# Fillers in one fp32r pass at both block heads, and block 2's first units in the scheduler's order

## The chip, the cores and the metric

The kernel runs on one core of a Trainium2 chip. The metric is the device time of one execution in microseconds, from its first to its last instruction and the little around it. Engines are named as in the profile: TensorE (PE, with PEld for its weight loads), VectorE (DVE), ScalarE (ACT), GpSimd (POOL) and SyncE (SP), which here only issues DMAs.

## The reference, cut to what matters

512 tokens of 2048 features go through three blocks in a row. Each block normalises, multiplies by a wide weight matrix, mixes the tokens in two ways, and multiplies by an output matrix.

```python
def reference(x, ...):                      # x: [1, 512, 2048], float32
    x = first_block(x, ...)
    x = second_block(x, ...)
    return third_block(x, ...)

def first_block(x, ...):
    h = rms_norm(x, norm_gain)
    z = einsum('bsd,de->bse', h, w_in)      # gated recurrence + dilated attention
    ...
    x = x + einsum('bse,ed->bsd', y, w_out)
    return rms_norm(x, final_gain)

def second_block(x, c, ...):
    shift, scale, gate = split(silu(c) @ w_ada + b_ada, 3)
    h = _layernorm(x) * (1.0 + scale) + shift
    proj = h @ w_in                         # spatial gating + neighbourhood attention
    ...
    x = _layernorm(x + (1.0 + gate) * y, ln_g, ln_b)

def third_block(x, c, ...):
    h = rms_norm_3(x, norm_gain) * (1.0 + scale) + shift
    ... = split(h @ w_in)                   # gated delta rule + sliding-window attention
    ...
    x = x + gate * (mixed @ w_out)
```

The change lies at the two places where one block ends and the next begins: the norm ahead of block 2, and the two norms ahead of block 3.

## The kernel before

**Tiles.** Activations are kept transposed, features on the 128 partitions and the 512 tokens along the row, so 2048 features are KT = 16 feature tiles of 128x512. Inputs and weights are float32. For the wide products each value is split into a high half, rounded to the type fp32r, and a low half, the rest. A weight piece is loaded by SP as `wr`, ACT rounds it to `wh` (L114, the helper `act`), DVE subtracts to get `wl` (L117, the helper `tt`). There are three buffers for `wr` and five each for `wh` and `wl`. An activation tile `a` is a pair (high, low) made in the same way. Each weight tile of 128x128 then takes three products of 128x512 (`mm`, L128): high x high, high x low, low x high. A unit is one 128-feature output tile: 16 feature tiles x 3 products into one PSUM bank `pm`.

**First units.** At the head of a block the activation tiles come one by one, since each must first be normalised. `first_units` (L231 to L279) therefore runs four units at once, tile by tile: when feature tile k is ready, its 4 x 3 products are issued. Only the last four tiles are taken unit by unit. `make(k)` is the work of one tile. For block 2 (L773 to L783) it is: two DVE operations `t <- t, x` with the broadcast norm factors, one ACT operation `t <- t` with the modulation's scale and bias, one on ACT for the high half, and one on DVE for the low half. `first_chunks` issues the loads of the weight pieces for tile k and splits them, through SP, ACT and DVE. `FIRST2 = (8, 0, 16, 9)` and `FIRST3` name the four units.

**Heads of blocks.** `out1` multiplies block 1's result by its output matrix, 16 units. Each unit's tile gets the residual, is normalised by the token means found so far, and is squared for the statistics. The last unit is in `out1_end`: its last products, its tile, sums over features by one-column products against `ones` (`stat_last`), then a chain of small operations on DVE and POOL that gives the norm's factors g and c, then `bcast_cols`, eight products of 128x128 that spread g and c over the partitions into the banks that `make` reads. `out2_end` does the same for block 3 with two norms in one, a longer chain, and three factors.

**Fillers.** In these two stretches TensorE has to wait for the others, and the kernel issues products whose results nobody reads. `warm(n, src)` issues n of them into a bank `x`. With `src = ds[0]`, a normalised float32 tile, each is a float32 product of `ones` and 512 columns. There are three groups at each head: behind the last unit, behind the sums, and behind the broadcasts.

**What sets the order.** Normally a scheduler orders the instructions of each engine by its own estimates. Inside `with self.in_order()` the instructions of DVE, ACT and TensorE stay in the order in which the code is written; SP and POOL are ordered by the scheduler throughout. Before the change, `out1_end` and the first units of block 2 that it calls were both inside (L725 and L726). `out2_end` with the first units of block 3 is inside as well, in both versions.

```python
    def run(self):
        ...
        h, first = self.out1(self.block1())
        h, first = self.out2(self.block2(h, first))
        self.drain_bg()
        self.out3(self.block3(h, first))
```

Of the kernel before, what the change touches and what calls it, by code (L numbers as in the profile page):

```python
# [18 lines left out]
P = 128  # L19
# [15 lines left out]
FIRST2 = (8, 0, 16, 9)  # L35
# [5 lines left out]
class Kernel:  # L41
# [148 lines left out]
    def warm(self, n, src=None):  # L190

        b = self.x()
        src = self.ones if src is None else src
        for _ in range(n):
            self.mm(b[:, 0:src.shape[-1]], self.ones, src)

    def in_order(self):

# [518 lines left out]
    def out1(self, ys):  # L717
        ysp = [self.split(v) for v in ys]
        self.stat_begin(3)
        ds = []  # L720
        self.sc2 = self.cp.tile([P, 32], F32, name="sc2")
        for ct in range(KT - 1):
            self.out1_tile(ct, self.unit(self.A["wo1"], ct, ysp), ds)
        self.ts(self.sc2, self.mod2[:, 16:48], 1.0, None, OP.add)
        with self.in_order():  # L725
            return self.out1_end(ysp, ds)  # L726

    def out1_tile(self, ct, ps, ds):
        nc = self.nc
# [19 lines left out]
    def out1_end(self, ysp, ds):  # L749
        nc = self.nc  # L750
        last, ps = self.last_unit(self.A["wo1"], ysp, self.stat_sum)
        self.warm(5, ds[0])
        lasts = self.out1_tile(KT - 1, last, ds)
        self.stat_last(ps, lasts)
        self.warm(5, ds[0])
        m, v, a, g, c = (self.s(4) for _ in range(5))

        self.ts(a, ps[:, 8:12], LN_EPS / D, LN_EPS * EPS)
        self.ts(m, ps[:, 0:4], 1.0 / D)
        self.stt(v, ps[:, 4:8], 1.0 / D, a, OP.mult, OP.add)  # L760
        self.tt(c, m, m)
        self.tt(v, v, c, OP.subtract)
        nc.gpsimd.tensor_tensor(g, v, self.nhalf[:, :4], OP.pow)
        self.r1 = self.cp.tile([P, 4], F32, name="r1")
        self.ts(a, ps[:, 8:12], 1.0 / D, EPS)
        nc.gpsimd.tensor_tensor(self.r1, a, self.nhalf[:, :4], OP.pow)
        self.stt(c, m, -1.0, g, OP.mult, OP.mult)
        chunks = self.end(self.first_chunks(self.A["w2"], FIRST2, 0))
        gb, cb = self.bcast_cols(g), self.bcast_cols(c)
        self.warm(5, ds[0])  # L770
        mod = self.mod2

        def make(k):  # L773
            t1 = self.t()
            self.tt(t1, ds[k], gb)
            self.tt(t1, t1, cb, OP.add)
            self.act(t1, t1, AF.Identity, scale=self.sc2[:, k:k + 1], bias=mod[:, k:k + 1])
            hi, lo = self.a(), self.a()
            self.act(hi, t1)
            yield  # L780
            yield
            self.tt(lo, t1, hi.bitcast(F32), OP.subtract)
            return hi, lo  # L783

        return self.first_units(self.A["w2"], FIRST2, make, chunks)


    def sgu(self, g, h, w, ys):
# [195 lines left out]
    def out2_end(self, ysp, ds, acc, cf, K, gsc, bsc):  # L984
        nc = self.nc
        mod = self.mod3
        w = self.A["w3"]

        def late():
            st = self.x()  # L990
            for i, a in enumerate(acc):
                for j in range(4):
                    self.mm(st[:, 5 * j + i:5 * j + i + 1], a[:, j * P:(j + 1) * P], self.ones[:, 0:1],
                            start=i == 0 and j == 0, stop=False)
            return st

        last, st = self.last_unit(self.A["wo2"], ysp, late)
        self.warm(4, ds[0])
        d, sq = self.out2_tile(KT - 1, last, ds, acc, cf)
        for v, o, n in ((d, 0, 3), (sq, 3, 2)):  # L1000
            for j in range(4):
                self.mm(st[:, 5 * j + o:5 * j + o + n], v[:, j * P:(j + 1) * P], cf[:, 0:n, KT - 1],
                        start=False, stop=True)
        self.warm(9, ds[0])
        s20 = self.s(20)
        nc.vector.tensor_copy(s20, st[:, 0:20])
        S = [s20[:, i::5] for i in range(5)]
        m, v, q, p, al, be = (self.s(4) for _ in range(6))
        g, c = self.gc3[:, 0:4], self.gc3[:, 4:8]
        self.ts(m, S[0], 1.0 / D)  # L1010
        self.ts(v, S[3], 1.0 / D, LN_EPS)
        self.tt(q, m, m)
        self.tt(v, v, q, OP.subtract)
        nc.gpsimd.tensor_tensor(g, v, self.nhalf[:, :4], OP.pow)

        self.ts(q, q, K[:, 0:1])
        self.tt(q, q, S[4], OP.add)
        self.tt(al, m, S[1])
        self.stt(q, al, -2.0, q, OP.mult, OP.add)
        self.stt(be, m, K[:, 1:2], S[2], OP.mult, OP.subtract)  # L1020
        self.tt(q, q, g)
        self.stt(q, be, -2.0, q, OP.mult, OP.add)
        self.tt(q, q, g)
        self.ts(q, q, K[:, 2:3], None, OP.add)
        nc.gpsimd.tensor_tensor(p, q, self.nhalf[:, :4], OP.pow)
        self.stt(c, m, -1.0, g, OP.mult, OP.mult)
        self.tt(al, g, p)
        self.tt(be, c, p)
        chunks = self.end(self.first_chunks(w, FIRST3, 0))
        rows = [self.k(t) for t in ("acc0", "km", "acc1")]  # L1030
        for r, v in zip(rows, (al, be, p)):
            b = self.bcast_cols(v)
            self.act(r, b)
        self.warm(5, ds[0])
        alb, beb, pb = rows

        def make(k):
            t1 = self.t()
            self.tt(t1, ds[k], alb)
            self.tt(t1, t1, beb, OP.add)  # L1040
            self.act(t1, t1, AF.Identity, scale=gsc[:, k:k + 1], bias=mod[:, k:k + 1])
            yield
            self.stt(t1, pb, bsc[:, k:k + 1], t1, OP.mult, OP.add)
            hi, lo = self.a(), self.a()
            self.act(hi, t1)
            yield
            self.tt(lo, t1, hi.bitcast(F32), OP.subtract)
            return hi, lo

        small = []  # L1050
        for n in range(4):
            small.append(self.x())
        W = 272

        def side(k, h):

            raw = self.t()[:, :W]
            nc.sync.dma_start(raw, self.A["w3s"][:, k * W:k * W + W])
            hi, lo = self.e(F32R)[:, :W], self.e(F32R)[:, :W]
            self.act(hi, raw)  # L1060
            yield
            self.tt(lo, raw, hi.bitcast(F32), OP.subtract)
            yield
            for n in range(4):
                c, o = slice(n * P, (n + 1) * P), small[n][:, :W]
                self.mm(o, h[k][0][:, c], hi, start=k == 0, stop=False)
                self.mm(o, h[k][1][:, c], hi, start=False, stop=False)
                self.mm(o, h[k][0][:, c], lo, start=False, stop=k == KT - 1)

        h, first = self.first_units(w, FIRST3, make, chunks, side)  # L1070
        self.vb = [self.rows1, self.cp.tile([P, T], F32, name="vb1")]
        self.ba = self.cp.tile([P, 64], F32, name="ba")
        for n in range(4):
            nc.vector.tensor_copy(self.ba[:, 16 * n:16 * n + 16], small[n][:, 256:272])
            for i in range(2):
                self.act(self.vb[i][:, n * P:(n + 1) * P], small[n][:, i * P:(i + 1) * P])
        return h, first
# [678 lines left out]
```

## Time and profile before

| | |
|---|---|
| median of 3 runs | 3457.22 us (3456.98 to 3463.95) |
| the profiled execution | 3459.73 us |
| its span, first to last instruction | 3458.0 us |
| its mean granted TensorE clock | 0.996 |
| products of `pm` with `wh`, with `wl` | 8512, 4256 |
| DMA | 451.68 MB, mean 131 GB/s |

The page gives busy time by engine, and a list of the costliest groups of instructions with the idle time ahead of them and the engine that ended it. Busy time alone says little here, since TensorE is nearly always busy, some of it with fillers. The views that matter are the list of waits on TensorE, the busy time by stretches of the span, and the instructions one by one around the two block heads, which lie near 1045 to 1063 us and 1966 to 1985 us. A row such as `pm <- DVE a L117` reads: a product into `pm` waited for the tile `a`, which DVE writes on line 117. Numbers in the order below are buffer numbers of the program; the profile leaves them out.

### The profile page before, as it was taken

What the parts mean: (1) busy time and instruction counts of PE and PEld (TensorE: products, weight loads), DVE (VectorE), ACT (ScalarE), POOL (GpSimd) and SP (SyncE); (2) the same over time, 40 slices, a digit from 0 to 9 for tenths busy, and PEclk for the clock granted to TensorE, in tenths of its full rate; (3) what the DMA queues carried; (4) which work ended last, traced back from release to release, by engine and by line L of the source; (5) the groups of instructions that cost most, each with busy time, mean ns of one, the idle gap of its engine ahead of it and who ended that gap; (6) DMA issues with size and microseconds to landing.
All of it is one profiled execution on the core that took longest, in us unless ns stands there. A gap on an engine that the chain in (4) does not pass through costs nothing.

```text
span 3458.0 us, 44442 instructions
## 1 busy us (share of the span) xinstructions
PE 3408.4 (99%) x16689; PEld 2827.2 (82%) x16689; DVE 1976.9 (57%) x3593; ACT 1278.8 (37%) x2459; POOL 132.8 (4%) x156
## 2 busy tenths in 40 slices
PE   9999999999998999999999999999999999999999
PEld 7877788888885888888888788888888888888887
DVE  8677656657775556644357677756754333344552
ACT  4222244445334222544452243332334443432331
POOL 0000000000000000101000000000000000000000
PEclk9999999999999999999999999999999999999999
DMA  6355445435662355432234233332222233324442
GB/s 220 124 181 177 135 140 178 157 117 185 213 217 93 129 166 200 169 124 90 88 101 144 95 111 106 99 98 84 84 71 84 96 101 104 126 98 146 140 139 96
DMA packets 166168, 451.68 MB, mean 131 GB/s; under 512 B 26496, under 2 KB 47296, under 8 KB 165952
## 3 DMA queue, kind: packets, MB, share of 16 engines
q1 hardware_dynamic: 165952, 448.84, 39.6%
q8 instruction: 131, 2.15, 0.3%
q14 instruction: 85, 0.70, 0.1%
HBM read 423.58 MB, written 25.18 MB: 130 GB/s over the span
## 4 chain that ended last, share of the span: by engine, by line
PE 53%; DVE 4%; issue 1%; ACT 1%; POOL 0%; DVEq 0%; ACTq 0%; POOLq 0%
PE pm L128 46%; PE x L128 6%; DVE fp L117 1%; PE x L614 1%; PE x L134 1%; DVE wl L117 1%; DVE ft L1275 1%; DVE t L117 1%; DVE t L120 0%; ACT t L114 0%; POOL s L142 0%; ACT wh L114 0%; DVE s L1380 0%; DVE s L117 0%; DVE ex_p L120 0%
## 5 line engine op out<-in xcount | busy, mean ns | idle before, releaser
L128 PE MATMUL pm<-a,wh 128*128 128x512 f32 x8512 | 2673.3, 395 | 16.6 <-DVE a L117 14.0
L128 PEld LDWEIGHTS pm<-a,wh 128*128 128x128 f32 x8512 | 1574.5, 189 | 338.5 <-DVE a L117 20.2
L128 PE MATMUL pm<-a,wl 128*128 128x512 f32 x4256 | 1666.3, 392 | 0.5 <-DVE wl L117 0.5
L114 ACT ACTIVATE wh<-wr 128x512 fp32r<-128x512 f32 (+2 forms) x1073 | 671.4, 627 | 1716.3 <-PE pm L128 1626.4
L117 DVE TENSOR_TENSOR wl<-wr,wh 128x512 fp32r<-128x512 f32 (+2 forms) x1073 | 740.4, 692 | 987.8 <-ACT wh L114 921.1
L128 PEld LDWEIGHTS pm<-a,wl 128*128 128x128 f32 x4256 | 801.2, 188 | 172.6 <-DVE wl L117 0.9
L120 DVE SCALAR_TENSOR_TENSOR ga<-gr,sc_c,ga 128x1024 f32<-128x1024 f32 x180 | 231.4, 1286 | 85.6 <-DMA gr<-in_wada_dram 85.0
L114 ACT ACTIVATE t<-x 128x512 f32<-128x512 f32 (+3 forms) x317 | 150.5, 489 | 105.5 <-PE x L128 47.9
L128 PEld LDWEIGHTS x<-t,t 128*128 128x128 f32 (+3 forms) x1296 | 155.6, 183 | 28.5 <-issue 6.6
L114 ACT ACTIVATE t<-t 128x512 f32<-128x512 f32 (+2 forms) x204 | 125.0, 613 | 140.0 <-DVE t L117 92.7
L128 PE MATMUL x<-t,t 128*128 128x64 f32 (+5 forms) x1296 | 167.2, 273 | 5.2 <-DVE t L117 5.2
L117 DVE TENSOR_TENSOR t<-t,t 128x512 f32<-128x512 f32 (+2 forms) x233 | 155.8, 669 | 21.8 <-ACT t L114 18.4
L114 ACT ACTIVATE t<-t,s 128x128 f32<-128x128 f32 (+2 forms) x192 | 98.5, 514 | 81.2 <-DVE s L525 62.2
L142 POOL TENSOR_TENSOR s<-s,nhalf 128x4 f32<-128x4 f32 (+1 forms) x51 | 60.8, 1192 | 1279.1 <-DVE s L125 1272.7
L614 PE MATMUL x<-cst,t 128*128 128x128 f32 x464 | 74.7, 275 | 4.7 <-ACT t L114 4.7
L134 PE MATMUL x<-cst,t 128*128 128x128 f32 x464 | 70.3, 274 | 6.4 <-DVE t L117 3.5
L134 PEld LDWEIGHTS x<-cst,t 128*128 128x128 f32 x464 | 56.5, 140 | 22.2 <-DVE t L117 3.4
L128 PE MATMUL x<-acc,t 128*128 128x128 f32 (+3 forms) x336 | 72.9, 310 | 0.0
L120 DVE SCALAR_TENSOR_TENSOR t<-t,pm 128x512 f32<-128x512 f32 x64 | 43.7, 684 | 46.2 <-PE pm L128 46.0
L117 DVE TENSOR_TENSOR a<-t,a 128x512 fp32r<-128x512 f32 x96 | 63.9, 686 | 9.3 <-ACT a L114 9.1
L114 ACT ACTIVATE t<-pm 128x512 f32<-128x512 f32 (+2 forms) x154 | 68.9, 482 | 0.2
L614 PEld LDWEIGHTS x<-cst,t 128*128 128x128 f32 x464 | 56.7, 152 | 9.9 <-ACT t L114 6.1
(228 smaller groups left out, 1667.0 us busy)
## 6 DMA issues: line engine op xcount, KB each, us to landing
wr<-in_w_dram SPq DMA_DIRECT2D x380, 512.0 KB, 3.4
gr<-in_wada_dram SPq DMA_DIRECT2D x192, 512.0 KB, 4.2
wr<-in_wo_dram SPq DMA_DIRECT2D x96, 512.0 KB, 3.4
t<-in_xt_dram SPq DMA_DIRECT2D x32, 256.0 KB, 3.9
res<-t SPq DMA_DIRECT2D x32, 256.0 KB, 2.0
t<-res SPq DMA_DIRECT2D x32, 256.0 KB, 2.7
gld<-t SPq DMA_DIRECT2D x32, 256.0 KB, 2.0
t<-gld SPq DMA_DIRECT2D x32, 256.0 KB, 2.8
```

The costliest lines, as they stand in the source:

```text
L114: return self.nc.scalar.activation(out, in_, fn, **kw)
L117: return self.nc.vector.tensor_tensor(out, a, b, op)
L120: return self.nc.vector.scalar_tensor_tensor(out, a, s, b, op0=op0, op1=op1)
L128: return self.nc.tensor.matmul(out, l, r, start=start, stop=stop, skip_group_check=True)
L134: self.nc.tensor.transpose(b[:, p * P:(p + 1) * P], src[:, p * P:(p + 1) * P], self.ident)
L142: self.nc.gpsimd.tensor_tensor(out, u, self.nhalf[:, :n], OP.pow)
L614: self.nc.tensor.transpose(b[:, j * P:(j + 1) * P], pr[:, j * P:(j + 1) * P], self.ident)
L1275: nc.vector.tensor_reduce(tv[:, :, i], pv, AX, OP.add, negate=True)
```

## The change

Two things change. `warm` with a source now multiplies fp32r by fp32r: the high half of the sixteenth tile of the block's output operand, `ysp[15][0]`, gives both the 128 weight columns and the 512 moving columns. The groups get other counts: 5, 5, 5 become 10, 8, 9 ahead of block 2, and 4, 9, 5 become 9, 17, 12 ahead of block 3. Without a source `warm` issues the same products as before. And `out1_end` returns the arguments of `first_units` in place of calling it; `out1` calls it after the `with`, so the scheduler orders the first units of block 2.

```diff
     def warm(self, n, src=None):
         b = self.x()
-        src = self.ones if src is None else src
         for _ in range(n):
-            self.mm(b[:, 0:src.shape[-1]], self.ones, src)
+            if src is None:
+                self.mm(b[:, 0:P], self.ones, self.ones)
+            else:
+                self.mm(b, src[:, 0:P], src)
...
         with self.in_order():
-            return self.out1_end(ysp, ds)
+            args = self.out1_end(ysp, ds)
+        return self.first_units(self.A["w2"], FIRST2, *args)
...
     def out1_end(self, ysp, ds):
         last, ps = self.last_unit(self.A["wo1"], ysp, self.stat_sum)
-        self.warm(5, ds[0])
+        self.warm(10, ysp[15][0])
         lasts = self.out1_tile(KT - 1, last, ds)
         self.stat_last(ps, lasts)
-        self.warm(5, ds[0])
+        self.warm(8, ysp[15][0])
...
         gb, cb = self.bcast_cols(g), self.bcast_cols(c)
-        self.warm(5, ds[0])
+        self.warm(9, ysp[15][0])
...
-        return self.first_units(self.A["w2"], FIRST2, make, chunks)
+        return make, chunks
...
     def out2_end(self, ysp, ds, acc, cf, K, gsc, bsc):
-        self.warm(4, ds[0])
+        self.warm(9, ysp[15][0])
...
-        self.warm(9, ds[0])
+        self.warm(17, ysp[15][0])
...
-        self.warm(5, ds[0])
+        self.warm(12, ysp[15][0])
```

The order of instructions changes only around these two places. First TensorE at the head of block 2, before: the last product of block 1's output, the fillers (`t`, `ones`), the sums over the last tile (`ones`, `t`, one column), fillers, the broadcasts of g and c (`cst` is the identity), fillers, and the first products of block 2.

```order
L128 MATMUL pm1445_8711<-a1266_7356,wl1451_8753 128x512
L128 MATMUL x1453_8793<-t1282_7448,ones_87 128x512 x5
L128 MATMUL x1452_8768<-ones_87,t1455_8802 128x1 x4
L128 MATMUL x1452_8768<-ones_87,t1456_8805 128x1 x4
L128 MATMUL x1452_8768<-ones_87,t1457_8806 128x1 x4
L128 MATMUL x1458_8821<-t1282_7448,ones_87 128x512 x5
L128 MATMUL x1470_8864<-cst_84,s1462_8830 128x128 x4
L128 MATMUL x1471_8869<-cst_84,s1463_8831 128x128 x4
L128 MATMUL x1472_8874<-t1282_7448,ones_87 128x512 x5
L128 MATMUL pm1474_8881<-a1478_8888,wh1465_8844 128x512
L128 MATMUL pm1474_8881<-a1479_8889,wh1465_8844 128x512
L128 MATMUL pm1474_8881<-a1478_8888,wl1465_8845 128x512
```

The same place on TensorE in the changed kernel (`a1266` is the high half of the sixteenth operand tile; `a1478` and `a1479` are the two halves of block 2's first tile):

```order
L128 MATMUL pm1445_8711<-a1266_7356,wl1451_8753 128x512
L128 MATMUL x1453_8793<-a1266_7356 128x512 x10
L128 MATMUL x1452_8768<-ones_87,t1455_8807 128x1 x4
L128 MATMUL x1452_8768<-ones_87,t1456_8810 128x1 x4
L128 MATMUL x1452_8768<-ones_87,t1457_8811 128x1 x4
L128 MATMUL x1458_8826<-a1266_7356 128x512 x8
L128 MATMUL x1470_8872<-cst_84,s1462_8838 128x128 x4
L128 MATMUL x1471_8877<-cst_84,s1463_8839 128x128 x4
L128 MATMUL x1472_8882<-a1266_7356 128x512 x9
L128 MATMUL pm1474_8894<-a1478_8901,wh1465_8852 128x512
L128 MATMUL pm1475_8895<-a1478_8901,wh1466_8856 128x512
L128 MATMUL pm1476_8896<-a1478_8901,wh1467_8860 128x512
```

The fillers have another source and other counts, in the same three places. Of the first tile, the high-half products of the four units now come first, and those with the low half behind them; from the second tile on the products stand as before.

Next DVE in the middle of block 2's first units, before. `x1470` and `x1471` hold the broadcast g and c; each cycle has one weight's low half, the two operations of one tile, and the low half of the tile before.

```order
L117 TENSOR_TENSOR wl1519_9087<-wr1518_9084,wh1519_9086 128x512
L117 TENSOR_TENSOR t1520_9102<-t1384_8249,x1470_8864 128x512
L117 TENSOR_TENSOR t1520_9102<-t1520_9102,x1471_8869 128x512
L117 TENSOR_TENSOR a1517_9081<-t1515_9076,a1516_9080 128x512
L117 TENSOR_TENSOR wl1524_9113<-wr1523_9110,wh1524_9112 128x512
L117 TENSOR_TENSOR t1525_9128<-t1395_8337,x1470_8864 128x512
L117 TENSOR_TENSOR t1525_9128<-t1525_9128,x1471_8869 128x512
L117 TENSOR_TENSOR a1522_9107<-t1520_9102,a1521_9106 128x512
```

The same tiles on DVE in the changed kernel:

```order
L117 TENSOR_TENSOR t1520_9115<-t1384_8249,x1470_8872 128x512
L117 TENSOR_TENSOR t1525_9141<-t1395_8337,x1470_8872 128x512
L117 TENSOR_TENSOR t1520_9115<-t1520_9115,x1471_8877 128x512
L117 TENSOR_TENSOR wl1514_9074<-wr1513_9070,wh1514_9073 128x512
L117 TENSOR_TENSOR a1512_9067<-t1510_9062,a1511_9066 128x512
L117 TENSOR_TENSOR a1517_9094<-t1515_9089,a1516_9093 128x512
L117 TENSOR_TENSOR t1525_9141<-t1525_9141,x1471_8877 128x512
L117 TENSOR_TENSOR wl1519_9100<-wr1518_9097,wh1519_9099 128x512
L117 TENSOR_TENSOR t1530_9167<-t1408_8433,x1470_8872 128x512
L117 TENSOR_TENSOR a1522_9120<-t1520_9115,a1521_9119 128x512
```

The two operations of a tile stand one to two tiles further ahead of the low halves than before: the low half `a1517` came right behind both operations of `t1520`, and now the first of `t1525` is ahead of it too; the weight's low half `wl1514` stands behind them.

Last SP at the end of block 2's first units, before: the last weight pieces of the first units (L215), the first of the next units (L156), and six small loads (`t1555`, `t1557`) for the spatial gating.

```order
L215 DMA wr1551_9261<-in_w2_dram 128x256
L215 DMA wr1553_9279<-in_w2_dram 128x128
L156 DMA wr1573_9361<-in_w2_dram 128x1024
L792 DMA t1555_9298<-in_wsT_dram 128x128
L795 DMA t1555_9298<-in_sgu_b_dram 128x128
L795 DMA t1555_9298<-in_b_sp_dram 128x128
L792 DMA t1557_9304<-in_wsT_dram 128x128
L795 DMA t1557_9304<-in_sgu_b_dram 128x128
L795 DMA t1557_9304<-in_b_sp_dram 128x128
L156 DMA wr1580_9413<-in_w2_dram 128x1024
```

The same place on SP in the changed kernel, whose lines are numbered two to three higher:

```order
L217 DMA wr1551_9274<-in_w2_dram 128x256
L795 DMA t1555_9310<-in_wsT_dram 128x128
L798 DMA t1555_9310<-in_sgu_b_dram 128x128
L798 DMA t1555_9310<-in_b_sp_dram 128x128
L795 DMA t1557_9316<-in_wsT_dram 128x128
L798 DMA t1557_9316<-in_sgu_b_dram 128x128
L798 DMA t1557_9316<-in_b_sp_dram 128x128
L217 DMA wr1553_9292<-in_w2_dram 128x128
L156 DMA wr1573_9373<-in_w2_dram 128x1024
L156 DMA wr1580_9425<-in_w2_dram 128x1024
```

Two weight loads, `wr1553` and `wr1573`, have moved behind the six small loads.

## The prediction

> **What bounds the kernel now.** I read the page's busy times first, then the list of who waited for whom on TensorE, then its busy time by stage. A row of the stage table gives the stretch in us, its length, busy time and instructions of PE, PEld, DVE, ACT and POOL, the granted clock, DMA share and GB/s.
>
> ```profile
> PE 3408.4 (99%) x16689; PEld 2827.2 (82%) x16689; DVE 1976.9 (57%) x3593; ACT 1278.8 (37%) x2459; POOL 132.8 (4%) x156
> PE pm L128 <- DVE a L117: 14.0, 13, 2.4
> 1062.49:1069.66 7.17, 6.25 (x28) 4.67 (x26) 5.16 (x8) 2.98 (x5) 0.00 (x0) 1.00 0.23 71
> 1069.66:1110.43 40.77, 30.31 (x121) 21.75 (x121) 25.78 (x40) 19.66 (x31) 0.00 (x0) 1.00 0.19 56
> 1110.43:1127.68 17.25, 14.42 (x48) 10.07 (x48) 7.87 (x14) 9.18 (x16) 0.00 (x0) 0.80 0.46 145
> 1127.68:1445.00 317.32, 316.19 (x1507) 263.84 (x1506) 191.86 (x346) 101.83 (x192) 21.95 (x20) 1.00 0.51 172
> ```
>
> TensorE is the bound nearly everywhere: the 317 us after the first units hold 1.1 us without it. So what is won ahead of such a stretch stays won. The largest wait of the program, 14.0 us in 13 pieces, lies wholly in block 2's first units (1062.49 to 1127.68), where DVE is busy only 25.78 of 40.77 us. A loaded engine is not waited for there; an order is:
>
> ```profile
> 1077.19 0.81 ACT L114 ACTIVATE t<-t,mod,sc 128x512 f32<-128x512 f32 x1 [2.08 <-DVE t L117]
> 1078.04 0.63 ACT L114 ACTIVATE a<-t 128x512 fp32r<-128x512 f32 x1
> 1078.58 0.62 ACT L114 ACTIVATE wh<-wr 128x512 fp32r<-128x512 f32 x1
> 1079.23 0.69 DVE L117 TENSOR_TENSOR wl<-wr,wh 128x512 fp32r<-128x512 f32 x1 [1.46 <-ACT wh L114]
> 1079.84 1.40 DVE L117 TENSOR_TENSOR t<-t,x 128x512 f32<-128x512 f32 x2
> 1081.16 0.69 DVE L117 TENSOR_TENSOR a<-t,a 128x512 fp32r<-128x512 f32 x1
> 1081.27 0.81 ACT L114 ACTIVATE t<-t,mod,sc 128x512 f32<-128x512 f32 x1 [2.08 <-DVE t L117]
> 1081.90 0.50 PE L128 MATMUL pm<-a,wh 128*128 128x512 f32 x1 [1.02 <-DVE a L117]
> ```
>
> ACT does t, a, wh; only then DVE does wl, both adds, and the low half a; only then ACT's next t. The two engines take turns: ACT's t starts every 4.08 us (1077.19, 1081.27). The low half's input was there at 1078.67, but it stands behind wl and two adds until 1081.16, and TensorE waits for it.
>
> What a product costs when nothing is waited for is in the chain that ended last:
>
> ```profile
> 1573.99 24.51 PE pm L128 x108
> ```
>
> 24.51 / 108 = 0.227 us each. A feature tile has 4 units x 3 = 12 products, 2.72 us, against a cycle of 4.08.
>
> **Part 1, block 2's first units in the scheduler's order.** It adds and removes no instruction; it moves DVE's, ACT's and, at its end, SP's. TensorE's order changes in the first tile alone: the four products of the high half stand first, 4 x 0.227 = 0.91 us of cover while the low half is computed. The 192 products take 1127.68 - 1062.49 = 65.19 us and need 192 x 0.227 = 43.6. The lost 21.6 us are 10 cycles of 4.08 less 2.72 (13.6), 17.25 less 48 x 0.227 at the end (6.4), and 7.17 less 24 x 0.227 at the start (1.7).
>
> Can the new order feed one tile each 2.72 us? A DVE operation over 512 columns lets the next start 0.61 us later (1079.23 to 1079.84). Per tile it has wl, two adds and a: 4 x 0.61 = 2.44. In the new order the two adds of a tile mostly stand apart, with another tile's work between, so an add seldom waits for the one before it. ACT has three, 0.85 + 0.54 + 0.54 = 1.93 by the starts above (the third taken like the second). Both are below 2.72, so TensorE becomes the bound, with DVE 10% behind it. DVE has some 59 operations from the first add on, 36.0 us. TensorE comes to the last four tiles after 144 products, 32.7 us after its first, and that one lies some 4 us behind DVE's first add. So DVE is through under 1 us before the last four tiles are begun, and the fourth's low half is needed ten products, 2.3 us, later still. I take the whole 21.6.
>
> The other queue that the step moves past is SP's:
>
> ```profile
> SPq L215 <- DVE wl L117: 53.4, 13, 7.6
> wr<-in_w_dram SPq DMA_DIRECT2D x8, 256.0 KB, 2.7
> 1112.70 0.42 SPq L792 DMA_DIRECT2D t<-in_wsT_dram  x1
> ```
>
> SP mostly waits for DVE's wl to free one of three raw buffers, 53.4 us in these units; a load then lands after 2.7 us. With three buffers and a tile each 2.72 us, a load has two tiles' time, 5.4 us, before its wl blocks DVE. At the end, six small loads for the next stage now issue ahead of two weight pieces, at 0.42 each 2.5 us. The wait that stands on them is for statistics sums done long before. I cost them at nothing: the last four tiles' 48 products, 10.9 us, cover them; without that cover they would cost up to the 2.5. The scaling of r1, a DVE operation on four columns, moves to the end and is not waited for before block 2's output.
>
> **Part 2, the fillers at the head of this stage.**
>
> ```profile
> 1045.55 4.45 PE L128 MATMUL x<-t,ones 128*128 128x512 f32 x10
> 1049.84 2.73 PE L128 MATMUL x<-ones,t 128*128 128x1 f32 x24
> 1052.43 4.54 PE L128 MATMUL x<-t,ones 128*128 128x512 f32 x10
> 1056.81 1.95 PE L128 MATMUL x<-cst,s 128*128 128x128 f32 x16
> 1062.49 1.02 PE L128 MATMUL pm<-a,wh 128*128 128x512 f32 x2
> 1046.93 0.75 DVE L120 SCALAR_TENSOR_TENSOR t<-t,par,t 128x512 f32<-128x512 f32 x1
> 1047.71 0.63 ACT L114 ACTIVATE t<-t 128x512 f32<-128x512 f32 x1 [0.15 <-DVE t L120]
> 1054.41 0.16 DVE L120 SCALAR_TENSOR_TENSOR s<-s,s 128x4 f32<-128x4 f32 x1 [1.11 <-POOL s L763]
> 1054.49 1.69 DVE L117 TENSOR_TENSOR wl<-wr,wh 128x128 fp32r<-128x128 f32 x4
> 1057.90 0.69 DVE L117 TENSOR_TENSOR t<-t,x 128x512 f32<-128x512 f32 x1 [1.64 <-PE x L128]
> ```
>
> Five fp32 fillers are ten passes, 4.29 us (1045.55 to 1049.84), 0.86 each. The new form has the two operand types of the main products and their width; no filler of that form ran. I take 0.227, the nearest row, with the old 0.86 as the other end.
>
> First group: 10 x 0.227 ends at 1047.82. The sums behind it need d (1047.68) and later the square (1048.34): they start at 1047.82, 2.02 us earlier, and end at 1050.41. Second group: 8 x 0.227 ends at 1052.23. The broadcasts need DVE's result, 1.98 us after the sums (1054.41 - 1052.43): about 1052.4 now. The fillers had held them until 1056.81, so 4.4 us go, and what is late next is the statistics chain. Then DVE: the four wl, moved up with the sums, leave it free at 1054.1; one more wl stands ahead of the adds now (to 1054.7); the first tile's second add ends at 1056.6, ACT does two t and then a (0.81 + 0.73 + 0.63), and the first product starts at about 1058.8 in place of 1062.49. **3.7 us.** The third group (9 x 0.227, to about 1056.2) lies beside that and costs nothing.
>
> **Part 3, the fillers ahead of block 3.**
>
> ```profile
> 1966.38 3.77 PE L128 MATMUL x<-t,ones 128*128 128x512 f32 x8
> 1969.99 1.84 PE L128 MATMUL x<-cf,t 128*128 128x3 f32 x16
> 1971.69 7.97 PE L128 MATMUL x<-t,ones 128*128 128x512 f32 x18
> 1979.50 2.84 PE L128 MATMUL x<-cst,s 128*128 128x128 f32 x24
> 1967.41 0.69 DVE L117 TENSOR_TENSOR t<-t,t 128x512 f32<-128x512 f32 x1
> 1975.72 0.24 DVE L117 TENSOR_TENSOR s<-gc,s 128x4 f32<-128x4 f32 x2 [1.06 <-POOL s L1025]
> 1975.87 1.69 DVE L117 TENSOR_TENSOR wl<-wr,wh 128x128 fp32r<-128x128 f32 x4
> 1981.22 0.69 DVE L117 TENSOR_TENSOR t<-t,acc 128x512 f32<-128x512 f32 x1 [3.66 <-ACT acc L114]
> ```
>
> Nine fillers end at about 1968.55 (the first at the half clock shown below); d is there at 1968.10; the sums move by 1.44 and end at 1970.25. The 17 end at 1974.1; the chain's result comes 4.2 us after the sums, at 1974.5. The broadcasts start there and not at 1979.50: **5.0 us.** DVE's first add follows by 1.72, at 1976.2; its four wl end at 1976.1, so they just do not hold it. The last group of 12 (2.7 us) ends before the first tile is ready.
>
> **The pause that is uncovered.** Between the third group and the first product TensorE now stands for about 2.6 us (1056.2 to 1058.8). A pause of that size is in the trace:
>
> ```profile
> 1114.27 0.79 PE L128 MATMUL pm<-a,wh 128*128 128x512 f32 x1 [2.44 <-DVE a L117]
> 1109.98:1113.40 3.42, 1.23 (x3) 0.48 (x3) 2.03 (x4) 1.69 (x3) 0.00 (x0) 1.00 0.04 11
> 1113.40:1116.81 3.41, 2.32 (x5) 1.29 (x5) 2.70 (x5) 2.65 (x4) 0.00 (x0) 0.50 0.65 205
> 1116.81:1120.22 3.41, 3.41 (x9) 2.21 (x8) 1.12 (x2) 1.78 (x3) 0.00 (x0) 0.50 0.22 58
> ```
>
> A stretch of 3.41 us with TensorE busy a third of it is followed by two at clock 0.50. That loss goes with its pause (it is in the 6.4). The new pause may bring one back: one such stretch at half clock loses 1.7 us, bounds 0 and 3.4. I take 1.7.
>
> The Trainium skill, "TensorE: Matmul & The Clock Gate", section "Why this matters for your kernels", asks for no gaps above about 3 us between bursts, so it would leave this one unpunished. By it the sum is 30.3 and not 28.6. The rows show a pause of 2.44 us punished, though with shorter ones beside it, and I side with them; the page's case is the third rival below.
>
> **Sum.** 21.6 + 3.7 + 5.0 - 1.7 = 28.6 us. The profiled execution took 3459.73 (span 3458.0 and 1.7 around it), so 3431.1; the median of the runs is 2.5 below it, so **3428.6**.
>
> **Rivals.** *DVE does not keep up*: its margin is 0.28 us per tile, and a wl that waits for its weights holds the adds behind it. If half of the cycles keep their 1.36 us (6.8), and the tail half of its 6.4, 10 us are missing: 3438.6. For it: the margin is thin. Against: a load has 5.4 us and lands after 2.7. *The fillers held nothing up*: the statistics were late anyway and only the stage gains, 21.6 - 1.7: 3437. Against: DVE's results stand ready at 1054.57 and 1975.96 (start plus duration of the two rows above), TensorE goes on at 1056.81 and 1979.50. *No half clock*: the new pause does not fall into one stretch as the old one did, because where the stretches begin is not tied to it; the 1.7 stays, 3426.9. For it: before, 24 products of one column (1049.84 to 1052.43) left TensorE nearly as empty for 2.6 us, and the clock stayed at 1.00 up to 1110.43. *Slower*: the new filler runs in two passes like the old, 0.86 each. The 27 + 38 fillers then take 55.9 us where the 15 + 18 old ones took 28.4, 27.5 more, all of it ahead of chains that wait, and 21.6 - 27.5 gives 3463.1. It turns at 0.77 us a filler. Against: 12,768 products of this type and width take 0.227.
>
> **Chances.** Forecast with one half-clock stretch 0.47, without it 0.25, DVE behind 0.15, fillers held nothing 0.06, slower 0.03, nothing to measure 0.02, a larger gain than any here 0.02. The range runs from the full-clock sum and a few us of half clock that go elsewhere, 3422, to just past the two partial cases, 3441. This kernel's measurement can tell 0.2%, 7 us, from no change: faster 0.95, within it 0.02, slower 0.03.
>
> **What would show it.** The wait of pm for DVE's a, 14.0 us, falls below 4; the 192 products take 44 to 47 us; the ten-pass fillers are single passes of 0.227; the broadcasts start 2.0 and 4.2 us behind the sums; one stretch of 0.50 near the first product or none. If the stage still shows a cycle near 4 us, part 1 is wrong; if fillers come in pairs, parts 2 and 3 are.

## The result, and the profile after

| | median us | runs | ratio to before, same chip (95%) |
|---|---|---|---|
| before | 3460.59 | 4 (3456.98 to 3466.5) | |
| changed | 3431.56 | 4 (3428.47 to 3432.8) | 0.9913 [0.9895, 0.9931] |

The change takes 29.0 us off; 28.6 were forecast, and 3431.56 lies 3.0 us above the 3428.6 of the prediction, inside its range. The profiled execution took 3428.47 with a span of 3426.8.

The page's busy time by engine, and from the list of TensorE's waits the two rows of products into `pm` that lie at the block heads (waited for, us in total, times, longest):

```profile
PE 3387.9 (99%) x16688; PEld 2826.3 (82%) x16688; DVE 1974.5 (58%) x3593; ACT 1277.3 (37%) x2459; POOL 133.1 (4%) x156
PE pm L128 <- ACT a L114: 3.5, 2, 2.2
PE pm L128 <- DVE a L117: 0.2, 1, 0.2
```

The wait for DVE's `a`, 14.0 us before, is 0.2. What is left at each block head is one wait for ACT's first high half. (Products into `pm` also wait 1.7 us for `wh` and 0.3 for `wl`, outside both heads; before it was 2.2 and 0.5.) The stage table around block 2's head (stretch, length, busy time of PE, PEld, DVE, ACT, POOL, clock, DMA share, GB/s):

```profile
1053.58:1059.86 6.28, 4.13 (x27) 3.40 (x26) 6.28 (x13) 2.10 (x4) 0.93 (x1) 1.00 0.36 125
1059.86:1105.12 45.26, 45.26 (x192) 37.24 (x193) 35.64 (x61) 31.24 (x50) 0.00 (x0) 0.96 0.36 110
1105.12:1430.00 324.88, 324.06 (x1554) 270.82 (x1553) 195.84 (x358) 106.23 (x204) 23.19 (x21) 1.00 0.50 170
```

The 192 products run without a gap from 1059.86 to 1105.12, DVE and ACT beside them. TensorE's rows at the two heads (start, duration, then the idle time ahead and who ended it):

```profile
1046.67 2.47 PE L128 MATMUL x<-a 128*128 128x512 f32 x10
1048.98 2.73 PE L128 MATMUL x<-ones,t 128*128 128x1 f32 x24
1051.57 2.11 PE L128 MATMUL x<-a 128*128 128x512 f32 x8
1053.58 2.05 PE L128 MATMUL x<-cst,s 128*128 128x128 f32 x16
1055.39 2.31 PE L128 MATMUL x<-a 128*128 128x512 f32 x9
1059.86 2.27 PE L128 MATMUL pm<-a,wh 128*128 128x512 f32 x5 [2.15 <-ACT a L114]
...
1942.05 2.20 PE L128 MATMUL x<-a 128*128 128x512 f32 x9
1944.09 1.84 PE L128 MATMUL x<-cf,t 128*128 128x3 f32 x16
1945.79 4.16 PE L128 MATMUL x<-a 128*128 128x512 f32 x17
1950.04 2.94 PE L128 MATMUL x<-cst,s 128*128 128x128 f32 x24
1957.03 0.50 PE L128 MATMUL pm<-a,wh 128*128 128x512 f32 x1 [1.32 <-ACT a L114]
```

Ten fillers are ten instructions and take 2.31 us (1046.67 to 1048.98); five took ten and 4.29 before. The stretches at half clock around the two heads in the same profile, and two full-clock ones ahead of them for comparison:

```profile
1039.67:1043.08 3.41, 3.41 (x29) 3.26 (x28) 1.99 (x2) 0.00 (x0) 0.00 (x0) 1.00 0.89 315
1043.08:1046.50 3.42, 3.42 (x10) 2.68 (x9) 1.28 (x1) 0.00 (x0) 0.00 (x0) 0.50 0.55 169
1056.74:1060.15 3.41, 1.26 (x6) 0.75 (x5) 3.41 (x7) 2.38 (x4) 0.00 (x0) 1.00 0.41 153
1060.15:1063.56 3.41, 3.41 (x9) 2.64 (x9) 3.10 (x6) 2.87 (x6) 0.00 (x0) 0.50 0.00 0
1937.38:1940.79 3.41, 3.41 (x11) 2.83 (x11) 0.00 (x0) 0.00 (x0) 0.53 (x1) 0.50 0.00 0
```

One of them (1060.15) follows the pause ahead of the first product. Stage by stage, from the starts of TensorE's rows in the two profiles:

| stage | before | after | difference | forecast |
|---|---|---|---|---|
| start to the fillers at block 2's head | 1045.55 | 1046.67 | +1.1 | 0 |
| fillers to broadcasts | 11.26 | 6.91 | -4.35 | -4.4 |
| broadcasts to first product | 5.68 | 6.28 | +0.6 | +0.7 |
| the 192 products | 65.19 | 45.26 | -19.9 | -21.6 + 1.7 |
| on to the fillers at block 3's head | 838.70 | 836.93 | -1.8 | 0 |
| fillers to broadcasts | 13.12 | 7.99 | -5.1 | -5.0 |
| broadcasts to first product | 6.57 | 6.99 | +0.4 | 0 |
| the rest | 1471.93 | 1469.77 | -2.2 | 0 |
| span | 3458.0 | 3426.8 | -31.2 | -28.6 |

### The profile page after: what moved, and what is told of

It reads as the page before. It is cut to its first block, busy times and chain, and to the rows that moved or that the text cites. A ratio compares the mean times of both kernels' runs of the same rounds, so it can differ in the third digit from the quotient of the medians.

```text
span 3426.8 us, 44441 instructions
## 1 busy us (share of the span) xinstructions
PE 3387.9 (99%) x16688; PEld 2826.3 (82%) x16688; DVE 1974.5 (58%) x3593; ACT 1277.3 (37%) x2459; POOL 133.1 (4%) x156
## 3 DMA queue, kind: packets, MB, share of 16 engines
q8 instruction: 131, 2.15, 0.3%
## 4 chain that ended last, share of the span: by engine, by line
PE 53%; DVE 4%; issue 1%; ACT 1%; POOL 0%; DMA 0%; SPq 0%; DVEq 0%; ACTq 0%; POOLq 0%
PE pm L128 46%; PE x L128 5%; DVE fp L117 1%; PE x L616 1%; PE x L134 1%; DVE wl L117 1%; DVE ft L1278 1%; DVE t L117 1%; DVE t L120 0%; ACT t L114 0%; POOL s L142 0%; ACT wh L114 0%; DVE s L1383 0%; DVE s L117 0%; DMA t<-in_w3s_dram 0%
```

## The experiments

All are compared with before on the same chip.

| | median us | before | ratio (95%) | the 192 products, us |
|---|---|---|---|---|
| order_only | 3440.16 | 3460.24 | 0.995 [0.9935, 0.9965] | 43.96 |
| fillers_only | 3452.85 | 3460.24 | 0.9983 [0.9974, 0.9992] | 67.54 |
| lead_by_hand | 3455.7 | 3460.24 | 0.9986 [0.9974, 0.9998] | 66.27 |
| wh_ahead | 3438.29 | 3460.24 | 0.995 [0.9932, 0.9968] | 49.65 |
| no_fillers | 3441.67 | 3460.41 | 0.9939 [0.992, 0.9958] | 45.33 |
| cover | 3430.97 | 3460.41 | 0.9909 [0.989, 0.9928] | 43.53 |
| old_form_counted | 3434.58 | 3460.41 | 0.9917 [0.9895, 0.9939] | 43.90 |
| wl_late | 3431.63 | 3460.41 | 0.9911 [0.9883, 0.9939] | 43.68 |
| changed_again | 3429.0 | 3461.11 | 0.9904 [0.9889, 0.9918] | 43.67 |
| cover_wl_late | 3424.5 | 3461.11 | 0.9891 [0.9877, 0.9904] | 43.69 |

### order_only: the order without the new fillers

```diff
@@ before: out1
         with self.in_order():
-            return self.out1_end(ysp, ds)
+            args = self.out1_end(ysp, ds)
+        return self.first_units(self.A["w2"], FIRST2, *args)
...
-        return self.first_units(self.A["w2"], FIRST2, make, chunks)
+        return make, chunks
```

> Only the first units of block 2 go to the scheduler's order; fillers and counts as before. Theory (the two parts are separate and add up): the 192 products take 43.6 to 45.3 us and not 65.2, the broadcasts still start 4.4 us behind the end of the sums, and the old third group of fillers (3.9 us) covers the wait for the first tile, so no stretch at half clock follows there. 20 to 21.6 us less than before, ratio near 0.994. Rival (the order needs the shorter head, since DVE starts later relative to TensorE): more than 50 us for the 192 products, ratio 0.996 or above.

The stage of the 192 products in this kernel:

```profile
1064.15:1108.11 43.96, 43.96 (x195) 36.16 (x194) 34.97 (x59) 31.08 (x49) 0.00 (x0) 1.00 0.36 114
```

The products take their own time and nothing else, at full clock: 21.2 us less than before. The old third group of fillers runs up to the first product, and no half clock follows. By the medians it takes 20.1 us off. The rival falls. The broadcasts missed the 4.4 us: they stood 6.1 us behind the end of the sums, since a stretch at half clock fell on the second group.

### fillers_only: the fillers without the order

```diff
@@ changed: out1 and out1_end
         with self.in_order():
-            args = self.out1_end(ysp, ds)
-        return self.first_units(self.A["w2"], FIRST2, *args)
+            return self.out1_end(ysp, ds)
...
-        return make, chunks
+        return self.first_units(self.A["w2"], FIRST2, make, chunks)
```

> Only the fillers change; block 2's first units stay in written order. Theory: the broadcasts come 4.35 us earlier at block 2 and 5.1 us earlier at block 3, the first products 3.8 and 4.7 us earlier; the 192 products keep their 65 us. 8 to 9 us less than before, ratio near 0.9975. Rival (the fillers held nothing that counts): ratio 0.9995 to 1.0005. Rival (what is won ahead is lost as half clock): 5 us or less.

From fillers to first product it takes 13.5 us at block 2 (16.9 before) and 15.2 at block 3 (19.7 before), 3.45 and 4.4 less, against 3.8 and 4.7 expected. The first units keep their length, and here lose 2.4 us more:

```profile
1055.86:1123.40 67.54, 51.85 (x193) 36.76 (x193) 39.51 (x63) 33.22 (x52) 0.00 (x0) 0.95 0.26 78
```

So at block 2 not all of the 3.45 is kept. From the first filler to the end of the first units it takes 81.0 us here and 82.1 before: 1.1 less. Before, the third group of fillers had itself held the first product (ACT's first high half starts at 1060.36, the product at 1062.49, 2.13 us later; here 0.68). In the written order the turns of DVE and ACT set the pace of what follows, and DVE's first add came only 2.0 us earlier behind the first filler (12.35 and 10.34).

By the medians 7.4 us are gained, by the ratio 5.9 with an interval from 2.8 to 9.0. That the fillers held nothing is excluded. The 8 to 9 expected lie at the upper end of the interval, and the second rival's 5 or less is not excluded; the profile's two heads give 1.1 + 4.4 = 5.5.

### lead_by_hand and wh_ahead: what it is in the order

The prediction gave two descriptions of the stall: the engines take turns, and the low half stands behind `wl` and two adds. These kernels part them. Both keep the written order. The first writes each tile's adds, `t` and high half one tile earlier; the second moves only ACT's `wh`.

```diff
@@ lead_by_hand: first_units, to which block 2 passes lead=1
+        for g in gens[:lead]:
+            next(g)
         for k in range(KT + 1):
...
-            if k < KT:
-                next(gens[k])
+            if k + lead < KT:
+                next(gens[k + lead])
```

> The change's fillers; block 2's first units stay in written order, but each tile's two adds, its t and its high half are written one tile earlier, so that the low half no longer stands behind the adds of the tile that follows it but has a full tile of lead. Theory 1 (TensorE waited because the low half stood behind wl and two adds): the cycle falls to 2.72 us, the 192 products take 44 to 47 us. Theory 2 (a ring through both engines sets the cycle: adds on DVE, then t, a and wh on ACT, then wl on DVE, which stands ahead of the next adds): the ring is as before, the cycle stays near 4.08 us and the 192 products take 60 to 65 us.

```diff
@@ wh_ahead: first_units, to which block 2 passes ahead=True
+            ch = None
+            if 0 < k < KT - 2:
+                ch = self.first_chunks(w, cts, k)
+                if ahead:
+                    next(ch)
             if k < KT:
                 next(gens[k])
...
-                if k < KT - 2:
-                    take(self.end(self.first_chunks(w, cts, k)))
+                if ch:
+                    take(self.end(ch))
```

> The change's fillers; block 2's first units stay in written order, but ACT's wh of a weight piece is written ahead of the t and a of the same tile and not behind them. DVE's order stays wl, two adds, low half. Theory 2 (the ring add, t, a, wh, wl, add): wl no longer waits for the t and a of its own round, the ring spans two rounds (4.08 / 2 = 2.04 us each), the products set the pace: cycle 2.72 us, 192 products in 44 to 47 us, as fast as the changed kernel within 3 us. Theory 1 (the low half's place on DVE): nothing is changed, 4.08 us a cycle and 60 to 65 us.

First the stage and, engine by engine, the cycle of lead_by_hand:

```profile
1057.67:1123.94 66.27, 49.40 (x192) 36.21 (x193) 39.19 (x63) 33.12 (x52) 0.00 (x0) 0.97 0.26 79
```

```profile
1079.27 0.81 ACT L114 ACTIVATE t<-t,mod,sc 128x512 f32<-128x512 f32 x1 [2.08 <-DVE t L117]
1080.12 0.63 ACT L114 ACTIVATE a<-t 128x512 fp32r<-128x512 f32 x1
1080.65 0.61 ACT L114 ACTIVATE wh<-wr 128x512 fp32r<-128x512 f32 x1
1083.35 0.81 ACT L114 ACTIVATE t<-t,mod,sc 128x512 f32<-128x512 f32 x1 [2.08 <-DVE t L117]
```

```profile
1081.30 0.69 DVE L117 TENSOR_TENSOR wl<-wr,wh 128x512 fp32r<-128x512 f32 x1 [1.46 <-ACT wh L114]
1081.91 1.40 DVE L117 TENSOR_TENSOR t<-t,x 128x512 f32<-128x512 f32 x2
1083.23 0.69 DVE L117 TENSOR_TENSOR a<-t,a 128x512 fp32r<-128x512 f32 x1
```

The low half has a whole tile of lead, and the cycle is still 4.08 us (1079.27 to 1083.35). The ring stands in these rows: `t` 0.85, `a` 0.53 and `wh` 0.65 to the start of `wl` at 1081.30, then 0.61 to the adds, then 1.44 to ACT's next `t`. `wl` waits 1.46 us for `wh`, and the adds, which need nothing of it, stand behind it. The stage and TensorE's waits of wh_ahead:

```profile
1059.96:1109.61 49.65, 46.22 (x192) 35.74 (x193) 38.87 (x63) 33.53 (x52) 0.00 (x0) 1.00 0.34 106
```

```profile
PE pm L128 <- DVE a L117: 2.0, 6, 0.6
PE pm L128 <- ACT a L114: 1.6, 4, 1.1
```

One instruction per tile, moved ahead on ACT, opens the ring and takes 15.5 of 65.2 us away with the order still written by hand. It falls short of the 44 to 47 expected and of the scheduler's 43.5 to 45.3. In its rows `wh` now waits ahead of `t`, for TensorE to free one of its five buffers:

```profile
1094.21 0.53 ACT L114 ACTIVATE wh<-wr 128x384 fp32r<-128x384 f32 x1 [1.40 <-PE pm L128]
1094.64 0.80 ACT L114 ACTIVATE t<-t,mod,sc 128x512 f32<-128x512 f32 x1
```

and 2.8 of TensorE's 3.6 us of waiting fall between 1095 and 1101, for that tile's `a` and the next ones. In the scheduler's order `wh` waits for TensorE too (1.48 us ahead of 1065.65), but there the next tile's `t` and high half stand ahead of it. By the medians, wh_ahead is 6.7 us above the changed kernel's 3431.56, not within the 3 expected; the stage alone gives 4.4 to 6.

### no_fillers, old_form_counted and cover: what the fillers do

The counts of old_form_counted are 3, 2, 5 and 2, 5, 5 in place of 10, 8, 9 and 9, 17, 12.

```diff
@@ no_fillers: warm
-            else:
-                self.mm(b, src[:, 0:P], src)
@@ old_form_counted: warm, and its calls
-                self.mm(b, src[:, 0:P], src)
+                self.mm(b, self.ones, src)
...
-        self.warm(10, ysp[15][0])
+        self.warm(3, ds[0])
...
@@ cover: behind the broadcasts of block 2, then of block 3
-        self.warm(9, ysp[15][0])
+        self.warm(18, ysp[15][0])
...
-        self.warm(12, ysp[15][0])
+        self.warm(18, ysp[15][0])
```

> The changed kernel without its 65 fillers at the two block heads. Theory (fillers hold nothing now and keep the clock up): the first products start no earlier than in the changed kernel, counted from the last unit's last product, and the sums, the broadcasts and the first products fall into stretches at half clock: four or more such stretches around the two heads against three, 4 to 10 us more than the changed kernel. Rival (the fillers are of no use once the order is right): the same time within 2 us, or less.

> The changed kernel with fillers of the old float32 form, but in counts that fill about the same time: 3, 2, 5 ahead of block 2 and 2, 5, 5 ahead of block 3 (0.86 us each). Theory (what held the broadcasts was the time of the fillers, not their type): the broadcasts stand as far behind the sums as in the changed kernel within 0.5 us, and the time is the same within 3 us. Rival (the type matters by itself, for the clock or for what the queue holds): 5 us or more above the changed kernel.

> The changed kernel with 18 fillers and not 9 behind the broadcasts of block 2, and 18 and not 12 ahead of block 3, so that the pause of 2.15 us ahead of the first product is filled. Theory (the pause costs half clock and nothing else): the first product comes at the same distance behind the sums (10.9 us, at most 0.3 more), and no stretch of 0.50 begins between 2 us ahead of it and 5 us behind it; the 192 products take 43.6 to 44.2 us; up to 1.7 us less than the changed kernel, which the runs alone may not tell. Rival (the fillers hold the first product): 1 us more or over.

These three ran on the same chip: 3441.67 (3437.82 to 3444.12), 3434.58 (3432.29 to 3437.36) and 3430.97 (3428.08 to 3433.09). Without fillers, the stage table and TensorE's rows at block 2's head:

```profile
1052.89:1063.13 10.24, 8.34 (x38) 8.26 (x39) 3.38 (x13) 2.59 (x6) 1.98 (x2) 0.50 0.26 95
```

```profile
1052.92 5.28 PE L128 MATMUL x<-ones,t 128*128 128x1 f32 x24 [2.40 <-DVE t L120]
1060.07 3.50 PE L128 MATMUL x<-cst,s 128*128 128x128 f32 x16 [1.87 <-POOL s L764]
1066.42 1.72 PE L128 MATMUL pm<-a,wh 128*128 128x512 f32 x3 [2.85 <-ACT a L114]
```

The sums take 5.28 us and not 2.73, the broadcasts 3.50 and not 2.05, since both run at half clock: they are on the path, so the fillers earn their place. The first product stands 16.3 us behind the start of the last unit's last product (13.5 in the changed kernel), around the two heads lie ten stretches of 3.41 us at half clock against three in the changed kernel's first profile, and the time is 10.7 us above cover, the nearest kernel of the three. Fillers of the old form in small counts put the broadcasts 4.6 us behind the start of the sums, as in the changed kernel (4.60). The time is 3.0 above it with intervals that overlap, and the profile has five such stretches around the heads against three. So what had held the broadcasts was the length of the groups; that the type does anything by itself is not shown.

cover has no wait of `pm` at block 2's head, and no half clock with the first product:

```profile
1058.08:1101.61 43.53, 43.53 (x194) 35.99 (x193) 34.70 (x60) 30.66 (x49) 0.00 (x0) 1.00 0.38 113
```

```profile
1056.63 1.14 ACT L114 ACTIVATE a<-t 128x512 fp32r<-128x512 f32 x2
1053.90 4.34 PE L128 MATMUL x<-a 128*128 128x512 f32 x18
```

The 1.7 us of the changed kernel's first profile are not lost here. But the first product stood 12.0 us behind the start of the sums and not 10.9, for two reasons. Another stretch at half clock (1049.57) lay on the second group and held the broadcasts 0.8 us longer, of which 0.4 remain at ACT's first high half. And the 18 fillers ran on past that half: the product starts 1.45 us behind it (1056.63 to 1058.08), against 0.67 in the changed kernel. So the rival is right for 0.8 us: 18 are too many here. The medians alone do not tell cover from the changed kernel, as expected.

### wl_late, cover_wl_late and changed_again: the rest of the head

```diff
@@ wl_late: out1 and out1_end
-            args = self.out1_end(ysp, ds)
-        return self.first_units(self.A["w2"], FIRST2, *args)
+            make, chunks = self.out1_end(ysp, ds)
+        return self.first_units(self.A["w2"], FIRST2, make, self.end(chunks))
...
-        chunks = self.end(self.first_chunks(self.A["w2"], FIRST2, 0))
+        chunks = self.first_chunks(self.A["w2"], FIRST2, 0)
+        next(chunks)
@@ cover_wl_late: as wl_late, and behind the broadcasts of block 2, then of block 3
-        self.warm(9, ysp[15][0])
+        self.warm(13, ysp[15][0])
...
-        self.warm(12, ysp[15][0])
+        self.warm(18, ysp[15][0])
```

> The changed kernel with the low halves of the first weight pieces no longer in written order behind the statistics chain, but where the scheduler puts them: three of them into the chain's own waits on DVE. Theory (the five low halves on DVE, 2.3 us, hold the first adds behind the broadcasts): the first add comes about 1 us earlier behind the sums, the first product 0.5 to 1 us earlier (10.9 to about 10.1 us behind the sums). Rival (they delay the chain itself): the broadcasts come later by 0.3 us or more and the first product gains nothing. A difference of this size is read from the trace and not from the times.

> The changed kernel with the first low halves of the weights where the scheduler puts them (as in wl_late), 13 fillers and not 9 behind the broadcasts of block 2 and 18 and not 12 ahead of block 3. Theory: the first product stands about 5.1 us behind the start of the broadcasts (6.3 in the changed kernel), TensorE's pause ahead of it is under 0.5 us, no stretch at half clock begins with it, the 192 products take 43.6 to 44 us: 1.2 to 2.9 us less than the changed kernel. Rival (the stretches at half clock fall elsewhere around the heads whatever stands there): the same number of them, and no difference beyond 1.2 us.

> The changed kernel once more, beside the one above, on the same chip. Theory (where the stretches at half clock begin is not tied to the program): its profile shows them at other places around the two heads than its first profile (1043, 1060 and 1937 us), and the time between the last unit's last products and the end of the first units differs by 1 to 3 us for that reason alone, with no other step of the chain changed by over 0.3 us. Rival (the program sets them): the same places within 1 us.

In wl_late, DVE's first add and TensorE's first product (broadcasts from 1054.80):

```profile
1054.80 1.95 PE L128 MATMUL x<-cst,s 128*128 128x128 f32 x16
1055.89 4.27 DVE L117 TENSOR_TENSOR t<-t,x 128x512 f32<-128x512 f32 x7 [0.49 <-PE x L128]
1059.90 0.50 PE L128 MATMUL pm<-a,wh 128*128 128x512 f32 x1 [1.10 <-ACT a L114]
```

The add stands 1.09 us behind the broadcasts (2.27 in the changed kernel, 1055.85 - 1053.58) and the first product 5.10 (6.28). Counted from the start of the sums it failed (11.3 us and not 10.1). The sums themselves took 0.4 us longer, in part at half clock. DVE's chain from its first to its last small operation took 2.28 us (1051.76 to 1054.04) and not 1.81, since low halves now stand between its steps: the rival has a share. And eight fillers, most at half clock, held the broadcasts another 0.7 us.

cover_wl_late, a version beyond the change, gave 3424.5 (3423.87 to 3426.61), 4.5 us less than the changed kernel beside it at 3429.0 (3427.0 to 3436.9). Its slowest of four runs lies below the fastest of the changed kernel's five, but the intervals of their ratios overlap, so a gain over the change is likely and not proved. Its product stage was as expected (43.69, pause 0.18 us); its first product stood 5.7 us behind the broadcasts, which ran partly at half clock. Around the two heads its profile has two stretches at half clock, the one beside it four.

changed_again shows stretches of 0.50 at other places around the two heads than the first profile (1043, 1060 and 1937 us):

```profile
1048.82:1052.23 3.41, 3.41 (x11) 2.73 (x11) 0.77 (x1) 0.00 (x0) 0.00 (x0) 0.50 0.78 244
1059.06:1062.48 3.42, 3.42 (x13) 2.94 (x12) 2.31 (x7) 0.00 (x0) 1.98 (x2) 0.50 0.03 4
1065.89:1069.30 3.41, 2.41 (x10) 1.91 (x11) 3.41 (x7) 3.38 (x7) 0.00 (x0) 1.00 0.00 0
1943.11:1946.52 3.41, 3.41 (x9) 2.67 (x10) 0.00 (x0) 0.00 (x0) 0.53 (x1) 0.50 0.00 0
1960.18:1963.59 3.41, 1.59 (x6) 0.78 (x6) 2.01 (x4) 2.50 (x5) 0.00 (x0) 1.00 0.23 75
1963.59:1967.00 3.41, 3.41 (x9) 2.63 (x9) 2.98 (x6) 1.70 (x3) 0.00 (x0) 0.50 0.37 118
```

The program has a share in where they fall. The first (1048.82) and the third (1943.11) stand 4.6 and 4.3 us ahead of the first filler of their head; in the first profile 1043.08 and 1937.38 stand 3.6 and 4.7 ahead. The other two are at other steps. Block 2's first product, at 1066.89, came after a pause too (1.1 us), but the stretch that holds it is busy for 2.41 of 3.41 us, and the clock stayed up; the 192 products took 43.67 against 45.26. At block 3 it is the other way round: the first product, at 1962.67, came after a pause of 1.59 us, in a stretch busy for 1.59 of 3.41, and half clock followed; in the first profile that pause was 1.32 us, its stretch (from 1954.44) busy for 1.88, and the clock stayed up. From block 2's first filler to the end of its first units it took 57.2 us here and 58.4 in the first profile, inside the 1 to 3 us of difference that were expected. The expectation that nothing else would move was too strict: the second group held the broadcasts 0.9 us longer here, and 0.5 of that came back behind them.

## Why the prediction was right

**Part 1, the order: right in size, and one of its two readings named a symptom.** 45.26 us with one half-clock stretch, 43.5 to 44.0 without, against 43.6 worked out. That the engines take turns was the cause. That the low half stands behind `wl` and two adds was true of the rows but not the cause: lead_by_hand freed it and kept the 4.08 us. The ring runs through `wh` and `wl`, and wh_ahead opened it there.

**DVE's margin of 0.28 us held.** The rival in which DVE does not keep up did not come: DVE is busy 35.64 of 45.26 us and TensorE does not wait for it once. The SP queue cost nothing there either.

**Parts 2 and 3, the fillers: right.** A filler took 0.23 us (2.31 / 10). The broadcasts moved by 4.35 and 5.1 against 4.4 and 5.0, the first products by 3.75 and 4.7 against 3.7 and 5.0. The 0.4 lost behind block 3's broadcasts was not in the sum, which left a load out. On ACT the rounding of a small weight piece (`in_w3s`) stands, as written, ahead of the first tile's high half, and now it waits for its load:

```profile
1955.33 0.43 ACT L114 ACTIVATE t<-t 128x272 fp32r<-128x272 f32 x1 [1.01 <-DMA t<-in_w3s_dram]
1955.66 0.80 ACT L114 ACTIVATE t<-t,mod,s 128x512 f32<-128x512 f32 x1
1956.37 0.61 ACT L114 ACTIVATE a<-t 128x512 fp32r<-128x512 f32 x1
```

SP issues that load behind the first weight pieces, 1.5 us ahead of the broadcasts before (1977.97) and 2.0 us behind them now (1952.07), since the broadcasts no longer wait for fillers. Before, ACT did not wait for it. (The half clock at block 3's first filler that the prediction takes as shown is the stretch from 1963.32 to 1966.73 of before, at 0.50; its rows show another one.) The slower rival's price of 0.86 us a filler is excluded, and that the fillers held nothing as well.

**The half clock: mechanism right, place a matter of chance.** The first profile has the forecast stretch, 1060.15 behind a pause of 2.15 us; the second has none there, but one at block 3's first product, behind a pause of 1.59 us. The Trainium skill, "TensorE: Matmul & The Clock Gate", section "Why this matters for your kernels", asks only for gaps of under about 3 us; both profiles disagree. The prediction saw that the last group ahead of block 3 ends before the first tile is ready and put that pause at nothing, without a reason. In the six profiles with 12 fillers there it lasts 1.3 to 1.8 us, and in five of them half clock follows the first product; that the first profile of the changed kernel is the sixth was luck. In the five profiles in which the group reaches up to the first product (before, order_only, old_form_counted, cover, cover_wl_late) none does.

The prediction put one such stretch at 1.7 us and left the others out of the sum. They moved too: -2.2 and -1.8 us of the profile's 31.2 lie in stages in which nothing that the change touches got shorter, and +1.1 ahead of block 2's head. Two half-clock stretches of before (2362.7 and 2574.3) are missing after.

**The sum.** The forecast was made against a before of 3457.22, the median of three runs; four give 3460.59. The gain was 29.0 for 28.6, and the 3.0 us between 3431.56 and 3428.6 are nearly that shift. In the profiles, the stages that the change touches give 28.4 of the 31.2.

## What to carry to other kernels

When two engines each wait for the other once a cycle, write the ring down instruction by instruction before moving anything: one instruction queued ahead of work that does not need it (`wl` ahead of the adds) closes it, and the operation that the bound engine waits for may be no part of it. Fillers ahead of a wait must end no later than the result that ends the wait, so count them from the trace; behind the last step, let them reach up to the first real product and not past it. When a step moves up, look also for loads that had landed in its shadow. And a gain below 5 us in a kernel whose clock drops by chance is read from the stage, not from a few times.

## What the runs showed of the hardware that was not expected

Half clock comes on a grid. In the changed kernel's first profile the stretches begin at 1043.08, 1060.15 and 1937.38: 17.07 and 877.23 us apart, 5 and 257 times 3.4133. In changed_again 1048.82, 1059.06 and 1943.11 are 3 and 259 such steps apart. The Trainium skill, "TensorE: Matmul & The Clock Gate", section "What's actually happening", calls the clock's window free-running and 3413 ns long; both profiles agree. The grid lies elsewhere in each execution, so the same pause falls into one cell or is shared by two. Over the whole span the first profile has six cells at half clock, changed_again nine, and these two executions of one kernel took 3428.47 and 3436.9 us; three cells at 1.7 us are 5.1 of the 8.4 between them.

A cell does not have to be idle throughout. Around the heads, cells with TensorE busy for 1.26 and 1.59 of 3.41 us were followed by half clock, cells with 1.88 and 2.41 were not.

What the clock counts is not the profile's busy time. In cover_wl_late the stretch ahead of a drop looks fully busy:

```profile
1045.94:1049.35 3.41, 3.41 (x28) 3.25 (x28) 0.89 (x6) 2.26 (x6) 0.00 (x0) 1.00 0.48 187
1049.35:1052.76 3.41, 3.41 (x12) 2.90 (x11) 2.15 (x7) 0.00 (x0) 2.23 (x2) 0.50 0.23 77
```

It holds the 24 one-column sums, 2.6 us long, and the next stretch runs at 0.50. The same stands in the changed kernel's rows 1039.67 and 1043.08. In both, products of one column were followed by half clock as if TensorE had stood still. Yet they do not seem to count for nothing: before, the cell from 1048.55 to 1051.96 held 2.12 us of the same sums beside 1.29 us of fillers, and no drop followed. That such products count for little is inferred from these places and was not tried by itself.
